# A hybrid decoder block on one core: the instruction order is planned from revised estimates of durations

## The chip, the core and the metric

The kernel runs on one core of a Trainium2 chip. The core's engines work side by side, each taking its own instructions strictly in program order: TensorE (PE) multiplies matrices and transposes, VectorE (DVE), ScalarE (ACT) and GpSimd (POOL) work elementwise, SyncE (SP) issues the DMA transfers. An instruction whose operands are not there yet holds up everything behind it on its engine. The metric is the device time of one execution in microseconds (us), as a median over runs.

## What is computed

One decoder layer, batch 1, 1024 tokens, model width 1024, all float32. Both token mixers read one normed input through one projection:

```python
xn = rms_norm(x, norm1_g)
q, k, v, p_rw = jnp.split(xn @ w_in, [512, 1024, 1536], axis=-1)   # p_rw: 1792 columns
attn = dilated_attention(q, k, v, q_norm_g, k_norm_g)    # 8 heads of 64; windows 128, 512, 2048 at dilation 1, 4, 16
attn = rms_norm(attn, attn_out_g)                        # per head
rwkv = rwkv7_time_mix(p_rw, ...)                         # 8 heads of 64
x = x + jnp.concatenate([attn, rwkv], axis=-1) @ w_out
xn2 = rms_norm(x, norm2_g)
return x + (silu(xn2 @ w_gate) * (xn2 @ w_up)) @ w_down  # 2816 hidden columns
```

The recurrent mixer is, per head and token, `state = state * w + (state·a) b + v k`, `y = state·r`. The dilated attention normalizes q and k (QK-norm), adds a linear bias, and joins three bands by their maxima and sums.

## The kernel before

**Arithmetic.** Matrix products take operands split in a high and a low part (names ending in h and l or hi and lo), so that one float32 product is three passes at the faster rate: `mm<-xn10h,inhi`, `xn10l,inhi`, `xn10h,inlo`.

**Stages.** (1) The start, 0 to 125 us: x is loaded in eight tiles `xt`, squared, normed, transposed (`norms`), and the first blocks of the in-projection (`inproj`, tiles `mm`) are made; `feed` takes each block's sums out: `wa` and `gl` for decays and gates, `stage` for the recurrence's r, k, v, and `sqf` (squares), `qs` (scaled copy), `exf` (the norm's factors, spread) and `vf` for q, k, v. (2) 125 to 567 us: the recurrence goes through the tokens block by block as matrix products; `chain` carries the state `S` from block to block (tiles `Rb`, `VS`, `Ub`; PE results in the `chain` banks), `invert` and `scoring` prepare its matrices, and the rest of the in-projection fills PE between. `post` turns the chain's `Y` into the mixer's output and stores it to DRAM as `mix_d`. (3) 567 to 855 us: attention; q, k, v go through DRAM (`qh_d`, `ql_d`, `kh_d`, `kl_d`, `v_d`) and each head's `qv`, `kk`, `vv` and `bias` are loaded again, seven attend workers make scores (`kk,qv`), softmax (`sb`) and PV products (`pt`), and the out-projection (`outproj`, 16 steps, weights `woraw` split into `woh`, `wol`) uses them: its first round takes the recurrent half, loaded as `mixr` from `mix_d`; the residual `acc` and the second norm (`norms2`, `T1h`, `T1l`) follow. (4) From 855 us the FFN (`gates`, `hidden`, `down`).

**What sets the order.** No order is written by hand. Every operation is handed by a generator (a "stream" with a rank) to a planner, the class `Flow`. It keeps an estimated clock for each engine and an estimated end for each buffer's last write and reads. `scan` gives each operation a cost from its engine and shape; `ready` works out when its operands are there (the end of the writer plus `LAG` of the writer's engine); `run` takes again and again the stream whose next operation is ready first, ties by rank, and `issue` advances the engine's clock and emits it. All instructions are emitted in one line, 229 (`op.fn(*op.a, **op.k)`), so the line tells nothing in the trace and groups are told apart by the names of tiles. The estimates have no effect on the chip but through the order, and through which of a pool's buffers or PSUM banks a tile gets. Banks are handed out by `Get` and given back by `Free` in the planned time. Streams are run in four parts: `flow.run(rwkv)` with the recurrence and the input side, `flow.run(dense)` with the last in-projection, then attention with the out-projection, then the FFN. A stream of a later part can't be emitted before the earlier part is planned to its end; the loads of `woraw`, `mixr` and `acc` come after the last store of `mix_d`. SP has a queue of its own in the plan: 475 ns for an issue, and the bytes at 360 per ns behind each other.

Of the kernel before, what the change touches and what calls it, by code (L numbers as in the profile page):

```python
# [44 lines left out]
NFIX = C_MASK  # L45


LAG = {"PE": 200, "ACT": 145, "DVE": 140, "POOL": 65, "SP": 900}

OWN = {"PE": 0, "ACT": 100, "DVE": 130, "POOL": 95, "SP": 900}  # L50


# [4 lines left out]
class Op:  # L57


    def __init__(self, eng, name, fn, a, k):  # L60
        self.eng, self.name, self.fn, self.a, self.k = eng, name, fn, a, k
# [40 lines left out]
class Flow:  # L102
# [4 lines left out]
    def __init__(self):  # L107
        self.now, self.clk, self.marks, self.streams = 0.0, {}, {}, []
        self.slots, self.keys, self.count, self.shared = {}, {}, {}, set()
        self.free, self.weights = {}, 0.0  # L110

    def tile(self, pool, shape, dtype, name, tag=None, bufs=1):
        tag = tag or name
# [13 lines left out]
    def scan(self, op):  # L127

        def size(ap):
            n = 1  # L130
            for d in ap.shape[1:]:
                n *= d
            return n

        args = [("out" if i == 0 else "in", v) for i, v in enumerate(op.a)] + list(op.k.items())
        aps = [(k, v) for k, v in args if hasattr(v, "tensor")]
        op.wr = [self.keys[v.tensor.name] for k, v in aps if k in ("out", "accum_out") and v.tensor.name in self.keys]
        op.rd = [self.keys[v.tensor.name] for k, v in aps if k not in ("out", "accum_out") and v.tensor.name in self.keys]
        op.wr += [k for k in op.rd if k[0] in self.shared]
        n = max(size(v) for k, v in aps)  # L140
        ptr = sum(hasattr(op.k.get(k), "tensor") for k in ("scale", "bias", "scalar", "scalar1"))
        if op.eng == "PE":
            if op.name == "transpose":
                op.cost, op.m = 110, 128
            else:
                n, m, k = size(op.k["out"]), size(op.k["lhsT"]), op.k["lhsT"].shape[0]
                passes = 1 if op.k["lhsT"].dtype != F32 else PASSES if max(m, k) <= 64 else 4
                op.cost, op.m = 0.4167 * n * passes + 3, m
        elif op.eng == "SP":
            op.cost = 0  # L150
            op.bytes = 4 * max(size(v) * v.shape[0] for k, v in aps)
        elif op.eng == "POOL":
            op.cost = (280 if op.k.get("op") == ALU.pow else 100) + 93 * ptr + n * (168 if op.k.get("op") == ALU.pow else
                                            {"tensor_tensor": 2.15, "tensor_copy": 3.4}.get(op.name, 1.1))
        elif op.eng == "ACT":
            op.cost = 95 + 0.83 * n + 93 * ptr + 91 * ("accum_out" in op.k)
        else:
            op.cost = 65 + 1.04 * n + 64 * ptr

    def advance(self, s):  # L160
        while s.head is None and not s.done:
# [14 lines left out]
    def ready(self, s):  # L176
# [11 lines left out]
        for keys, which in ((op.rd, 0), (op.wr, 0), (op.wr, 1)):  # L188
            for k in keys:
                if k in self.slots:  # L190
                    for e, t in self.slots[k][which].items():
                        if e != op.eng or (e == "SP" and (keys is op.rd or which)):
                            r = max(r, t + LAG[e] + (60 if op.eng == "PE" else 0))
                        elif keys is op.rd and which == 0:
                            r = max(r, t + OWN[e])
        return r

    def issue(self, s, r):
        op = s.head
        s.head = None  # L200
        if isinstance(op, Wait):
            return
        if isinstance(op, Get):
            free = self.free[op.kind]
            s.gift = sorted(free, key=free.get)[:op.n or 1]
            for tag in s.gift:
                del free[tag]
            if op.n is None:
                s.gift = s.gift[0]
            return  # L210
        start = max(r, self.now)
        if op.eng == "SP":
            self.clk["SP"] = start + 475
            end = max(start + 1125, self.clk.get("queues", 0.0)) + op.bytes / 360
            self.clk["queues"] = end
        else:
            if op.eng == "PE":

                start = max(start, self.weights + 0.833 * op.m)
                self.weights = start  # L220
            self.clk[op.eng] = end = start + op.cost
        for keys, which in ((op.rd, 1), (op.wr, 0)):
            for k in keys:
                self.slots.setdefault(k, ({}, {}))[which][op.eng] = end
        s.t = end + (LAG["SP"] if op.eng == "SP" else 0)
        self.emit(op)
# [1611 lines left out]
```

## Time and profile before

| | us |
|---|---|
| runs | 1501.85, 1491.08, 1494.26 (median 1494.26) |
| profiled execution | 1502.63 |
| its span in the trace | 1500.8 |
| its mean granted PE clock | 0.986 of full speed |
| PE busy / weight loads / DVE / ACT / POOL | 1420.0 / 1142.2 / 803.8 / 712.8 / 541.8 |
| 24737 instructions, DMA 173.83 MB | mean 116 GB/s |

The profiled execution lies above the median of the runs and at the upper end of them. A busy time is the sum of an engine's instructions, with overlaps counted once, so span minus busy time is the time in which the engine did nothing, for whatever reason. "Idle before ... <-releaser" names the instruction or transfer whose end came last before an engine went on.

### The profile page before, as it was taken

How to read it: one execution, taken by the hardware profiler on the slowest of the kernel's cores; microseconds unless marked ns; L12 is line 12 of the kernel's file. 1: busy time of each engine (PE TensorE's matmuls, PEld its weight loads, DVE VectorE, ACT ScalarE, POOL GpSimd, SP SyncE). 2: the span in 40 equal slices, each digit the busy share in tenths (PEclk: the TensorE clock that was granted, in tenths of full speed). 3: DMA queues.
4: the chain of work that ended last, by engine and by line, in shares of the span. 5: the costliest groups of instructions: out<-in, count | busy, mean ns of one | idle time of the engine just before them, and what ended most of it. 6: DMA issues, size and time to landing. Idle time of an engine off the chain costs nothing.

```text
span 1500.8 us, 24737 instructions
## 1 busy us (share of the span) xinstructions
PE 1420.0 (95%) x8710; PEld 1142.2 (76%) x8710; DVE 803.8 (54%) x1795; ACT 712.8 (47%) x1764; POOL 541.8 (36%) x564
## 2 busy tenths in 40 slices
PE   8899999999898998899899799999999999999999
PEld 6666766677676776788777688888888888888887
DVE  4456577765655345667687744344443444334334
ACT  6434646556667766557666533333333333333332
POOL 5432344345454455133436734444444440000000
PEclk9899999999999999999999899999999999999999
DMA  6242232331422338996813222222222223445443
GB/s 201 85 128 65 67 82 78 79 96 54 126 82 89 104 116 255 249 243 159 197 37 106 73 90 83 79 78 79 79 82 85 78 85 134 147 146 198 148 147 127
DMA packets 199789, 173.83 MB, mean 116 GB/s; under 512 B 39025, under 2 KB 150897, under 8 KB 199666
## 3 DMA queue, kind: packets, MB, share of 16 engines
q1 hardware_dynamic: 199666, 172.26, 38.7%
q8 instruction: 69, 1.13, 0.3%
q14 instruction: 54, 0.44, 0.1%
HBM read 130.26 MB, written 37.75 MB: 112 GB/s over the span
## 4 chain that ended last, share of the span: by engine, by line
PE 54%; DMA 4%; DVE 3%; SPq 1%; ACT 1%; issue 1%; POOL 0%; ACTq 0%; POOLq 0%; DVEq 0%
PE bank L229 26%; PE mm L229 15%; PE chain L229 13%; DMA kk<-kl_d 2%; SPq L229 1%; DMA bias<-in_tab_dram 1%; DMA qv<-qh_d 1%; DVE acc L229 1%; DMA acc<-in_x_dram 0%; DMA mixr<-mix_d 0%; DVE tt L229 0%; DVE ml L229 0%; DVE T1l L229 0%; DVE nxn L229 0%; POOL ro L229 0%
## 5 line engine op out<-in xcount | busy, mean ns | idle before, releaser
L229 ACT ACTIVATE oph<-fraw 128x512 fp32r<-128x512 f32 x208 | 126.6, 628 | 223.4 <-PE bank L229 117.6
L229 POOL TENSOR_TENSOR opl<-fraw,oph 128x512 fp32r<-128x512 f32 x76 | 101.4, 1336 | 210.6 <-PE bank L229 110.2
L229 DVE TENSOR_TENSOR opl<-fraw,oph 128x512 fp32r<-128x512 f32 x132 | 87.7, 689 | 143.3 <-ACT oph L229 143.3
L229 ACT ACTIVATE oph<-sw 128x512 fp32r<-128x512 f32 x80 | 50.6, 632 | 178.0 <-DVE sw L229 71.9
L229 POOL TENSOR_TENSOR inlo<-inraw,inhi 128x512 fp32r<-128x512 f32 x62 | 82.1, 1325 | 110.6 <-ACT inhi L229 101.0
L229 PE MATMUL bank<-oph 128*128 128x512 f32 x176 | 68.5, 389 | 0.0
L229 PE MATMUL bank<-opl,oph 128*128 128x512 f32 x176 | 68.5, 389 | 0.0
L229 PE MATMUL bank<-oph,opl 128*128 128x512 f32 x176 | 68.5, 389 | 0.0
L229 DVE TENSOR_TENSOR opl<-sw,oph 128x512 fp32r<-128x512 f32 x80 | 56.0, 701 | 18.7 <-ACT oph L229 18.7
L229 DVE SCALAR_TENSOR_TENSOR S<-chain,ec,Sp 64x64 f32<-64x64 f32 x112 | 31.6, 282 | 51.0 <-PE chain L229 40.9
L229 DVE TENSOR_TENSOR uu<-mm,uu 128x512 f32<-128x512 f32 x20 | 13.8, 692 | 81.4 <-PE mm L229 81.4
L229 ACT ACTIVATE Ub<-chain 64x64 f32<-64x64 f32 x128 | 28.2, 220 | 56.7 <-DVE VS L229 54.9
L229 POOL TENSOR_TENSOR sw<-fraw 128x512 f32<-128x512 f32 x40 | 51.9, 1298 | 0.0
L229 ACT ACTIVATE Y<-chain 64x64 f32<-64x64 f32 x128 | 27.2, 214 | 49.2 <-DVE S L229 36.2
L229 ACT ACTIVATE inhi<-inraw 128x512 fp32r<-128x512 f32 x62 | 38.7, 624 | 14.9 <-PE mm L229 7.0
L229 DVE COPY Rb<-chain 64x64 f32<-64x64 f32 x128 | 28.9, 226 | 27.9 <-PE chain L229 25.6
L229 POOL TENSOR_TENSOR up<-up,sg 128x512 f32<-128x512 f32 x20 | 32.5, 1627 | 30.0 <-POOL sw L229 16.0
L229 ACT ACTIVATE sb<-sb,mx 128x256 f32<-128x256 f32 (+3 forms) x64 | 36.3, 569 | 7.9 <-DVE mx L229 7.5
L229 POOL TENSOR_TENSOR rsf<-smf,nhalf 128x8 f32<-128x8 f32 x16 | 27.3, 1708 | 32.3 <-DVE smf L229 26.2
L229 PE MATMUL chain<-Rb,M 128*128 128x128 f32 x128 | 27.8, 299 | 11.7 <-DVE Rb L229 11.5
L229 PE MATMUL bank<-ra,kb 64*64 64x128 f32 x512 | 38.7, 277 | 0.0
L229 PEld LDWEIGHTS chain<-Rb,M 128*128 128x128 f32 x128 | 21.0, 188 | 23.2 <-DVE Rb L229 18.9
(485 smaller groups left out, 4219.4 us busy)
## 6 DMA issues: line engine op xcount, KB each, us to landing
fraw<-in_w_down_dram SPq DMA_DIRECT2D x88, 256.0 KB, 2.8
inraw<-in_w_in_dram SPq DMA_DIRECT2D x62, 256.0 KB, 3.0
fraw<-in_w_gate_dram SPq DMA_DIRECT2D x48, 256.0 KB, 3.7
fraw<-in_w_up_dram SPq DMA_DIRECT2D x48, 256.0 KB, 3.0
fraw<-h_d SPq DMA_DIRECT2D x44, 256.0 KB, 2.9
h_d<-up SPq DMA_DIRECT2D x42, 256.0 KB, 2.1
rkv_d<-stage SPq DMA_DIRECT2D x24, 256.0 KB, 2.3
xt<-in_x_dram SPq DMA_DIRECT2D x8, 512.0 KB, 7.2
```

Source lines behind the costliest of these rows:

```text
L229: op.fn(*op.a, **op.k)
```

## The change

`LAG["SP"]`, the time from a transfer's planned end until a reader may start, goes from 900 to 1500 ns. A new `SWITCH` of 100 ns is charged to PE when a product on the whole array (more than 64 rows and columns, and every transpose) follows one that isn't, or the other way round; it is charged when the operation is issued, and isn't looked at when streams are compared. Products in one pass cost 0.4375 ns for a column of the result instead of 0.4167. An ACT operation whose output has four dimensions (the regrouped copies of q, k, v) costs 1.9 ns for an element instead of 0.83. DVE's fixed part goes from 65 to 80 ns and its rate from 1.04 to 1.08, but 2.2 for scans and 2.0 for four dimensions.

```diff
-LAG = {"PE": 200, "ACT": 145, "DVE": 140, "POOL": 65, "SP": 900}
+LAG = {"PE": 200, "ACT": 145, "DVE": 140, "POOL": 65, "SP": 1500}
+SWITCH = 100
...
-        self.free, self.weights = {}, 0.0
+        self.free, self.weights, self.whole = {}, 0.0, True
...
             if op.name == "transpose":
-                op.cost, op.m = 110, 128
+                op.cost, op.m, op.whole = 110, 128, True
...
-                op.cost, op.m = 0.4167 * n * passes + 3, m
+                op.cost, op.m, op.whole = (0.4375 if passes == 1 else 0.4167) * n * passes + 3, m, min(m, k) > 64
...
-            op.cost = 95 + 0.83 * n + 93 * ptr + 91 * ("accum_out" in op.k)
+            rate = 1.9 if len(op.a[0].shape) == 4 else 0.83
+            op.cost = 95 + rate * n + 93 * ptr + 91 * ("accum_out" in op.k)
         else:
-            op.cost = 65 + 1.04 * n + 64 * ptr
+            rate = {"tensor_tensor_scan": 2.2}.get(op.name, 2.0 if len(aps[0][1].shape) == 4 else 1.08)
+            op.cost = 80 + rate * n + 64 * ptr
...
                 start = max(start, self.weights + 0.833 * op.m)
-                self.weights = start
+                if op.whole != self.whole:
+                    start += SWITCH
+                self.weights, self.whole = start, op.whole
```

Both kernels hold the same instructions: 7336 for PE, 1797 for DVE, 1454 for ACT, 569 for POOL and 898 for SP. Their order differs nearly everywhere up to the FFN, and hardly from there on. Three places follow.

The first is on PE near the end of the in-projection. `mm` is a block of the in-projection, `sqf` its squares made by ACT, `bank<-cs,sqf` their transposes (`cs` holds the identity). Before:

```order
L229 MATMUL mm_6421<-xn11h,inlo 128x512 x4
L229 MATMUL bank_6523<-cs,sqf_6489 128x128 x2
L229 MATMUL bank_6519<-cs,vf_6517 128x128 x4
L229 MATMUL bank_6523<-cs,sqf_6489 128x128 x2
L229 MATMUL mm_6525<-xn10h,inhi 128x512 x4
```

Now, from the end of the same block on:

```order
L235 MATMUL mm_6383<-xn11h,inlo 128x512 x2
L235 MATMUL mm_6481<-xn10h,inhi 128x512 x2
L235 MATMUL chain_6422<-Rb_115,M 128x128
L235 MATMUL mm_6481<-xn10h,inhi 128x512 x2
L235 MATMUL mm_6481<-xn10l,inhi 128x512 x4
L235 MATMUL bank_6499<-cs,sqf_6482 128x128 x4
```

The squares' transposes followed the last product of their own block at once; now eight products of the next block and one of the chain stand between.

The second is on PE from there to the first product on `mixr`, which opens the out-projection. `exf` is the spread norm factor of k, `woh` and `wol` are the out-projection's weights, and the chain's last product stands further ahead. Before:

```order
L229 MATMUL bank_6571<-cs,exf_6551 128x128 x4
L229 MATMUL mm_6525<-xn11l,inhi 128x512 x3
L229 MATMUL mm_6525<-xn11h,inlo 128x512 x4
L229 MATMUL bank_6618<-cs,mixr 128x128 x4
L229 MATMUL chain_6620<-cs,vf_6615 128x128 x4
L229 MATMUL chain_6636<-cs,mixr 128x128 x4
L229 MATMUL bank_6646<-woh_6511,mh 128x512
```

Now, from the chain's last product (`Ub,M`) on; `kk,qv` are scores of attention heads:

```order
L235 MATMUL chain_6422<-Ub_117,M 128x128
L235 MATMUL mm_6481<-xn11l,inhi 128x512 x4
L235 MATMUL mm_6481<-xn11h,inlo 128x512 x3
L235 MATMUL bank_6532<-cs,exf_6517 128x128 x4
L235 MATMUL mm_6481<-xn11h,inlo 128x512
L235 MATMUL bank_6561<-cs,vf_6559 128x128 x4
...
L235 MATMUL chain_6652<-kk,qv 128x256 x2
L235 MATMUL bank_6659<-kk,qv 128x512 x2
L235 MATMUL chain_6640<-kk,qv 128x384
L235 MATMUL mm_6666<-kk,qv 128x256 x2
L235 MATMUL chain_6640<-kk,qv 128x384
L235 MATMUL mm_6688<-cs,mixr 128x128 x4
```

The chain's last product moved into the middle of the last block of the in-projection, and scores of the first two heads (on 4096 columns, with three rows left out here) moved ahead of the first `mixr` product.

The third is on SP at the same place: the stores and loads in the order of issue. Before:

```order
L229 DMA kh_d<-qh_6453 128x512
L229 DMA mix_d<-Y 128x2x128
L229 DMA kl_d<-qs_6359 128x512
L229 DMA kk<-kl_d 64x512 x2
L229 DMA bias<-in_tab_dram 128x512
L229 DMA woraw<-in_w_out_dram 128x512 x5
L229 DMA v_d<-v_6532 128x2x256
L229 DMA v_d<-v_6533 128x2x256
L229 DMA mixr<-mix_d 128x512 x2
L229 DMA woraw<-in_w_out_dram 128x512
L229 DMA kh_d<-qh_6589 128x512
```

Now:

```order
L235 DMA v_d<-v_6472 128x2x256
L235 DMA v_d<-v_6473 128x2x256
L235 DMA kh_d<-qh_6548 128x512
L235 DMA kl_d<-qs_6486 128x512
L235 DMA mix_d<-Y 128x2x128
L235 DMA woraw<-in_w_out_dram 128x512 x5
L235 DMA mixr<-mix_d 128x512 x2
L235 DMA v_d<-v_6593 128x2x256
L235 DMA v_d<-v_6594 128x2x256
L235 DMA vv<-v_d 128x4x128
```

The last stores of k and the last but one of v moved ahead of the store of `mix_d`; between it and the load of `mixr` only the five loads of `woraw` are left. Further on, two loads of `acc` moved behind one head's loads, and the next five of `woraw` behind those of two more heads.

## Rows read from the trace of the kernel before

**Rows 1.** Page, part 1: busy us, share, instructions of each engine.

```profile
PE 1420.0 (95%) x8710; PEld 1142.2 (76%) x8710; DVE 803.8 (54%) x1795; ACT 712.8 (47%) x1764; POOL 541.8 (36%) x564
```

**Rows 2.** Stages: us, busy PE PEld DVE ACT POOL (instructions), PE clock, DMA share, GB/s.

```profile
0.00:125.00 125.00, 113.00 (x765) 82.02 (x766) 63.07 (x117) 57.37 (x101) 51.94 (x75) 0.93 0.43 131
125.00:567.00 442.00, 412.22 (x3639) 318.06 (x3638) 272.14 (x707) 274.65 (x849) 197.43 (x204) 1.00 0.30 87
...
584.00:815.00 231.00, 204.92 (x1283) 176.06 (x1284) 165.01 (x526) 144.26 (x421) 85.59 (x131) 0.97 0.68 180
815.00:855.00 40.00, 32.42 (x138) 25.43 (x137) 35.41 (x38) 24.83 (x44) 33.25 (x26) 0.87 0.22 66
855.00:1500.00 645.00, 642.10 (x2817) 528.58 (x2816) 259.68 (x395) 204.38 (x337) 164.11 (x123) 1.00 0.34 109
```

**Rows 3.** Waits of PE, 100 to 570: us in total, times, longest us.

```profile
PE chain L229 <- DVE Rb L229: 11.5, 15, 1.6
PE chain L229 <- ACT Ub L229: 4.0, 9, 0.8
PE bank L229 <- ACT sqf L229: 2.6, 5, 1.0
...
PE bank L229 <- ACT vf L229: 2.0, 4, 0.8
```

**Rows 4.** Waits of PE, 570 to 860.

```profile
PE bank L229 <- DMA mixr<-mix_d: 5.5, 1, 5.5
PE bank L229 <- DVE T1l L229: 3.3, 1, 3.3
PE mm L229 <- ACT first L229: 3.0, 1, 3.0
```

**Rows 5.** Timeline at 211: start us, us, instruction [idle before <-releaser].

```profile
211.36 0.30 PEld L229 LDWEIGHTS chain<-S,ra 128*128 128x128 f32 x2 [0.17 <-issue]
```

**Rows 6.** Timeline of PE in the start.

```profile
42.25 0.67 PE L229 MATMUL bank<-cs,xt 128*128 128x128 f32 x4 [2.07 <-DVE xt L229]
42.85 2.07 PE L229 MATMUL bank<-wa,w2a2s 64*128 64x512 f32 x2
```

**Rows 7.** Groups of ACT: count | busy us, mean ns | idle before.

```profile
L229 ACT ACTIVATE sqf<-mm 128x512 f32<-128x512 f32 x16 | 17.2, 1078 | 5.0 <-PE mm L229 4.5 <-issue 0.3
```

**Rows 8.** Timeline of PE at the handover to attention.

```profile
576.28 0.44 PE L229 MATMUL bank<-cs,sqf 128*128 128x128 f32 x2 [1.15 <-ACT sqf L229]
...
589.44 1.09 PE L229 MATMUL bank<-cs,mixr 128*128 128x128 f32 x4 [5.46 <-DMA mixr<-mix_d]
```

**Rows 9.** Chain that ended last, 560 to 590: start us, us, what.

```profile
563.72 0.44 PE bank L229 x4
...
566.45 0.24 PE chain L229 x2
566.69 4.33 PE mm L229 x19
...
582.96 6.35 DMA mixr<-mix_d
```

**Rows 10.** Timeline of SP's issues there.

```profile
576.58 0.38 SPq L229 DMA_DIRECT2D mix_d<-Y  x1
...
579.35 2.33 SPq L229 DMA_DIRECT2D woraw<-in_w_out_dram  x5
...
582.96 1.33 SPq L229 DMA_DIRECT2D mixr<-mix_d  x2
```

**Rows 11.** Windows in attention, columns as in rows 2.

```profile
580.00:590.00 10.00, 4.54 (x23) 3.56 (x22) 3.58 (x5) 5.49 (x9) 4.98 (x4) 0.94 1.01 314
590.00:600.00 10.00, 10.00 (x56) 8.98 (x55) 6.34 (x27) 7.37 (x21) 3.06 (x3) 0.88 0.85 276
680.00:760.00 80.00, 72.33 (x487) 63.41 (x486) 57.19 (x199) 54.29 (x167) 33.92 (x64) 0.96 0.69 166
720.00:730.00 10.00, 8.16 (x39) 7.59 (x39) 3.94 (x15) 3.99 (x12) 3.75 (x10) 0.66 0.97 229
```

## The prediction, made before the changed kernel ran

> **What bounds the kernel now.** I read the busy times first, then the stages, then the waits of TensorE (PE) stage by stage, then the chain that ended last around the places where the order changes. PE is busy for 1420.0 of the profiled execution's 1500.8 us, the next engine for 803.8 [rows 1]. So the kernel is bound by PE's work plus PE's holes, and a reordering that leaves the work as it is can move only the holes: 1500.8 − 1420.0 = 81 us at most, 5.4% of the time. The stages show where they lie [rows 2]: 12.0 us in the start (0 to 125 us), 29.8 in the recurrence (125 to 567), 26.1 in attention (584 to 815), 7.6 in the tail before the FFN (815 to 855), and only 2.9 in the FFN's 645 us. In the recurrence the holes belong to the chain of state products: PE waits 11.5 us in 15 places for Rb and 4.0 in 9 for Ub, and besides it 2.6 for sqf and 2.0 for vf [rows 3]. One wait of 5.5 us, for mixr, stands at the handover to attention, and in the tail there are 3.3 us for T1l and 3.0 for first [rows 4].
>
> **The change, part by part.** Nothing is added or removed: the same products, vector operations and transfers run, in another order. The new estimates have no cost on the chip. What is priced is where the order puts a wait.
>
> *FFN, from 855 us: 0.* Its order is practically the old one, and with 642.1 of 645.0 us busy [rows 2] no hole is left to shift.
>
> *Switches between 64-row and whole-array products: 0.* There are 162 on PE in the old order, 164 in the new. The row bounds one: the weights of a whole product after four small ones waited 0.17 us [rows 5], so two more cost less than 0.4 us. Below nothing isn't possible, as there are more of them.
>
> *Start: 0.* Here PE waits 2.07 us for xt at 42.25, and runs wa,w2a2s right after [rows 6]. The new order has the norms ahead of wa's Tanh on ScalarE (ACT), so the wait for xt goes and one for wa of about the same length comes in its place. Bounds: −2 (the old wait goes and none comes) to +4 (the new one is twice as long and in front of all that follows).
>
> *Feeds of q, k and v: −5.* An operation that squares or copies 512 columns in the regrouped 4-D form takes 1078 ns [rows 7]; the old table gives 95 + 0.83 × 512 = 520, the new one 95 + 1.9 × 512 = 1068. So the old order put the transposes of sqf and vf on PE too early: 9 of 16 times less than 1.4 us of other PE work stands between the product and the transposes of its squares, once nothing (the first order piece); in the new order it is 2 of 16, and for vf 1 of 8 instead of 7. The waits are 2.6 + 2.0 [rows 3] and the one of 1.15 at 576.28 [rows 8], 5.8 in all; one short place is left for vf and two for sqf, which I put at 0.8. Bounds −5.8 to 0.
>
> *The chain, 125 to 567: +4.* The longer estimates of the vector engines pull chain products apart in some places and crowd them in others. Adding up the PE work that covers each of the chain's steps, the mean rises (1.06 to 1.12 us ahead of the Rb product, 1.52 to 1.65 ahead of VS), but the thin places too: below 0.7 us 9 → 13 of 64 for Rb, below 0.9 us 7 → 12 of 64 for Ub, below 1.4 us 11 → 15 of 60 for S. At the mean wait of Rb and Ub in the rows (11.5 / 15 = 0.77 and 4.0 / 9 = 0.44 us [rows 3]), and S taken as Ub, that is 4 × 0.77 + 5 × 0.44 + 4 × 0.44 = 7.0; the thicker mean takes part of it back, and I keep about half. Bounds: +8, and −8 if the thicker mean halves the 15.5 us of these waits.
>
> *Handover to attention: +9.* This is the clearest change in the order. The chain's last product starts at 566.45 and the mixr product at 589.44 [rows 8, 9]; between them the old order has nearly the whole last in-projection (4.33 us for 19 products, 0.228 each [rows 9]), so PE is covered until 5.46 us before mixr lands. In the new order the chain's last product stands in the middle of the last mm block: behind it come 8 mm products (1.8 us), two groups of transposes (0.44 each [rows 9]), and then score products on 4096 columns (8 × 0.228 = 1.8), that is 4.5 us. The path to mixr itself: from the last chain product to the store of mix_d is 576.58 − 566.69 = 9.9 us; the store's own issue takes 0.38, the 5 issues of woraw that now follow it 2.33 [rows 10], and mixr lands 6.35 us after its issue [rows 9], 19.0 in all. 19.0 − 4.5 = 14.5 us of hole, against 5.5 before: +9. Bounds: 0, if the vector work behind the chain's end is shorter because fewer feeds stand in it; and +14, if mixr waits for mix_d's landing rather than for the queue: from 576.58 to 582.96 [rows 10] were 6.4 us, 3.7 more than my 2.7; and 1.8 for the scores, if their operands, which come through the same full queues (share 1.01, [rows 11]), are late and they cover nothing. What waits behind mixr on PE is the rest of the scores and the out-projection; nothing else can run, since the engine takes its instructions in order.
> The Trainium skill (DMA: Bandwidth & Descriptors, Anatomy of one DMA — SWDGE path) gives a transfer a fixed 2.0 us and 436 GB/s, an estimate of 2.6 us for mixr's 256 KB. The trace disagrees, with 6.35 us here [rows 9], so its term of about +5 in place of +9, and a sum of 1486, is not taken.
>
> *Attention and out-projection, 584 to 815: −8.* Scores start earlier: 59 us of PE work stand behind the last score product up to the norms instead of 44.5, so the heads' loads are spread over more time. Between 680 and 760 the 16 queues are idle for 31% of 80 us = 25 us [rows 11], while at 710 to 730 PE stands for the loads of the next head. The acc loads and the second five of woraw are behind two heads' loads in the new order. I take a third of the 25 us. Bounds: −25, and +10, when thinner covers count (median PE work ahead of the PV transposes 2.40 → 2.09 us, ahead of the sb ones 4.84 → 4.27: a tenth to an eighth less cover for 26 us of holes is +3, and I allow three times that).
>
> *Tail, 815 to 855: −4.* The first norm transposes stand 10 us of PE work earlier than in the old order, which is cover for the 7.6 us of holes there [rows 2], 6.3 of which are the two waits [rows 4]; half. Bounds −7.6 to 0.
>
> Sum: 0 + 0 + 0 − 5 + 4 + 9 − 8 − 4 = **−4 us**. The profiled execution took 1502.6 us, above the runs' median of 1494.26 (1491.08 to 1501.85); the difference carries over to the median: **1490 us**.
>
> **The rivals.**
> *Attention was paced by its loads, and is released (faster).* Speaks for it: the queues' 25 idle us between full stretches [rows 11], PE at 8.16 of 10 us in 720 to 730 with DMA at 0.97. Against: 205 of 231 us are PE work already [rows 2], so all 25 would have to come from the loads. Then −5 + 4 + 9 − 25 − 4 = −21, **1473 us**.
> *The long hole at the handover and thin covers (slower).* The mechanism is one: score and chain work that covered the handover now stands ahead of it. Where PE stood, the granted clock fell: 0.94 and 0.88 in the two stretches around the 5.5 us wait, 0.66 in 720 to 730 [rows 11], which is time at 1.2 instead of 2.4 GHz. In 590 to 600 a mean of 0.88 means 2.4 us at the lower level, some 1.2 us lost. The price: feeds −5, chain +4, handover +14, attention's covers +5, and 2 for the clock of a longer hole, with nothing from the tail: +20, **1514 us**. It decides if the hole at the handover is 15 us or more and attention gives nothing back.
> The Trainium skill (TensorE: Matmul & The Clock Gate, HAM oscillation) names the same: an idle PE drops to half clock and the next products start slow; the rows quoted show it.
> *The change doesn't do what it says.* The order is set by estimates, and PE waits by real latencies. If the new places of the feeds only turn waits for sqf into waits for chain products, −5 and +5 cancel, the handover's +9 stands against −8 of attention, and if the tail gives nothing either it is +1, **1495 us**. It lies within the forecast's case.
>
> **How the numbers follow.** Forecast and "no net change": 0.55 (0.05 of it the third rival). Faster rival 0.25, slower rival 0.20. A measurement of this kernel tells about 1% (15 us) from no change, so these are also the chances of faster, same and slower. The likeliest case's own range is 1480 to 1508. The range to be given reaches into the cases at both ends: 1473 is the released attention, 1512 just short of the slower one's whole price, which leaves out about 2 in 10.
>
> **What would show it.** Right: waits of PE for sqf and vf down from 5.8 to about 1; waits for Rb and Ub together at about 19 instead of 15.5; a hole of 12 to 16 us before the mixr product, with a granted clock under 0.9 behind it; FFN of 645 us as before; attention a little shorter, its last score product earlier. Wrong: if the hole at the handover stays near 5 us the term was too big and the time falls to some 1481; if these two fall below 11 us the covers were judged badly; if the FFN's length moves, nothing in this account explains it.

## The result

The changed kernel takes 1504.49 us as a median of 20 runs (1495.98 to 1509.59), the kernel before 1495.36 (1486.80 to 1506.00, 20 runs): a ratio of 1.0051 with a 95% interval of 1.003 to 1.0071. A second set of runs gave 1505.59 and 1496.04, 1.0076 (1.005 to 1.0102). So by its ratios it is some 8 to 11 us slower, clear of zero and inside what I had called "no change". The range held it; the sign was wrong, since 4 us of gain were forecast. Of the 89 runs of the kernel before that were made beside the experiments, one took 2297.60 us at a granted clock of 0.554 and is left out below.

The profiled execution of the changed kernel took 1504.73 us (span 1502.7). Its busy times answer to [rows 1], its stages to [rows 2]; columns are the same.

```profile
PE 1425.6 (95%) x8710; PEld 1147.0 (76%) x8710; DVE 805.3 (54%) x1795; ACT 710.4 (47%) x1764; POOL 537.3 (36%) x564
```

```profile
0.00:125.00 125.00, 112.78 (x707) 81.38 (x708) 60.74 (x115) 55.44 (x97) 52.65 (x75) 0.93 0.43 131
...
567.00:584.00 17.00, 11.84 (x61) 9.52 (x59) 8.01 (x19) 6.73 (x15) 3.89 (x3) 0.88 0.59 179
584.00:815.00 231.00, 208.33 (x1262) 174.49 (x1263) 162.76 (x523) 141.77 (x417) 81.62 (x131) 0.94 0.65 176
815.00:855.00 40.00, 32.67 (x140) 25.76 (x139) 35.12 (x37) 24.22 (x43) 30.66 (x24) 0.89 0.22 66
855.00:1500.00 645.00, 643.64 (x2819) 529.07 (x2817) 259.06 (x396) 204.89 (x338) 164.40 (x123) 1.00 0.34 108
```

The last row's window is a little later in the program than before, so it isn't the same work word for word, but two things stand out. PE is busy 5.6 us longer for the same products, with 3.7 us less of holes in the span; and the granted clock of attention is 0.94 instead of 0.97.

Waits of PE, as in [rows 3] (100 to 575 us), then as in [rows 4] (570 to 870), and last the waits for sb of the kernel before in 570 to 870:

```profile
PE chain L235 <- DVE Rb L235: 9.0, 13, 1.8
PE chain L235 <- ACT Ub L235: 8.0, 10, 1.8
```

```profile
PE mm L235 <- ACT sb L235: 5.7, 4, 3.4
PE mm L235 <- DMA mixr<-mix_d: 5.0, 1, 5.0
PE bank L235 <- DVE T1l L235: 3.4, 1, 3.4
PE bank L235 <- ACT first L235: 3.0, 1, 3.0
PE bank L235 <- ACT vf L235: 2.3, 1, 2.3
PE bank L235 <- DVE v L235: 2.0, 1, 2.0
...
PE bank L235 <- ACT sb L235: 1.8, 6, 0.5
PE chain L235 <- ACT sb L235: 1.8, 4, 0.7
```

```profile
PE mm L229 <- ACT sb L229: 0.9, 1, 0.9
...
PE bank L229 <- ACT sb L229: 0.6, 1, 0.6
```

The waits for sqf are gone and those for vf are one; the waits in the tail haven't moved. Waits for sb, attention's softmax, have grown from 1.5 to 9.3 us. The handover on PE, as in [rows 8], and on SP, as in [rows 10]:

```profile
577.15 0.66 PE L235 MATMUL bank<-cs,vf 128*128 128x128 f32 x4 [2.27 <-ACT vf L235]
...
580.86 1.19 PE L235 MATMUL bank<-kk,qv 128*128 128x512 f32 x2 [2.02 <-DVE v L235]
...
588.08 1.11 PE L235 MATMUL mm<-cs,mixr 128*128 128x128 f32 x4 [4.95 <-DMA mixr<-mix_d]
```

```profile
579.53 0.37 SPq L235 DMA_DIRECT2D mix_d<-Y  x1
580.00 2.33 SPq L235 DMA_DIRECT2D woraw<-in_w_out_dram  x5
582.37 1.21 SPq L235 DMA_DIRECT2D mixr<-mix_d  x2
```

Behind the chain's last product stood holes of 1.2, 0.4 and 5.5 us; now there are three of 9.2 us together, with 4.0 us of PE work between the first and the `mixr` product.

**Where the 9 us come from.** Windows cut at the same work, not at the same time, answer that: from the start of the first `mixr` product to the end of the last product of the second norm (`nxn`), which takes in all of attention and the out-projection. First the two profiles of the kernel before: that of [rows 1], and a second one (below), of a run 3 us above its median; then the changed kernel's. Columns as in [rows 2].

```profile
589.40:841.10 251.70, 228.00 (x1392) 194.61 (x1393) 183.54 (x543) 157.85 (x445) 104.22 (x147) 0.97 0.63 165
590.10:836.70 246.60, 229.39 (x1392) 195.86 (x1393) 182.47 (x543) 157.84 (x445) 104.16 (x147) 0.96 0.63 169
```

```profile
588.10:841.70 253.60, 232.04 (x1373) 193.73 (x1374) 181.61 (x531) 156.07 (x441) 100.07 (x147) 0.95 0.60 162
```

Against the second profile the changed kernel is ahead by 2.0 us up to this window (588.1 against 590.1), though the in-projection ends 9 to 10 us earlier (574.9 against 584.0 and 584.7 in the two profiles). In the window it takes 7.0 us more, and 19 products fewer stand in it. The rest, behind it, is 1.3 us longer. The first profile of before has 1.9 us less than the changed kernel in this window, so single profiles bound the loss there only loosely; the experiments below settle it.

### The profile page after: what moved, and what is told of

It is laid out like the page before. It is cut to its first block, busy times and chain, and to the rows that moved or that the text cites. A ratio compares the mean times of both kernels' runs of the same rounds, so it can differ in the third digit from the quotient of the medians.

```text
span 1502.7 us, 24763 instructions
## 1 busy us (share of the span) xinstructions
PE 1425.6 (95%) x8710; PEld 1147.0 (76%) x8710; DVE 805.3 (54%) x1795; ACT 710.4 (47%) x1764; POOL 537.3 (36%) x564
## 5 line engine op out<-in xcount | busy, mean ns | idle before, releaser
L235 DVE TENSOR_TENSOR up<-chain,uu 128x512 f32<-128x512 f32 x40 | 27.7, 692 | 29.7 <-PE chain L235 29.7
L235 PEld LDWEIGHTS bank<-oph 128*128 128x128 f32 x176 | 33.0, 188 | 6.9
L235 PEld LDWEIGHTS bank<-opl,oph 128*128 128x128 f32 x176 | 33.0, 188 | 6.8
L235 PEld LDWEIGHTS bank<-oph,opl 128*128 128x128 f32 x176 | 33.0, 188 | 6.8
```

## Experiments

All ratios are to the kernel before on the same chip. "Attention window" is the window just described; "first round" is the out-projection's first round, which uses the recurrent half. Positions "in us of PE work" come from adding up the products of the planned order, as in the prediction.

**A second look at both kernels.** The kernels as they are.

> The changed kernel as it is, beside the others on the same chip. Both theories expect what was measured: 1.005 of the kernel before (1.003 to 1.007), a mean granted clock about 0.98 against 0.986 in the profile of before. Theory C (clock): in its profile PE's busy time is about 5 us above that of before, with fewer holes. Theory H (holes): holes make up the difference.

> The kernel before, once more, for a second profile of it: the first was of an execution 7 us above the median of its runs. 1.000. If the in-projection again ends near 584 us, the changed kernel's end of it at 575 is a gain of 9 us that is lost later; if it ends near 578, the gain is some 3 us and so is what is lost later.

Measured: 1.0076 (1.005 to 1.0102) for the changed kernel; 0.9981 (0.9954 to 1.0008) for before against itself. In-projection's end 575.5 and 584.7, so its earlier end is not luck of one profile. Attention windows 253.1 against 246.6; in the first profile of before it was 251.7, 5.1 us more, about the 4.4 us by which that execution was longer than the second. In these profiles holes are equal (74.8 and 75.0 us over the span); what grew is PE's busy time, 1428.1 against 1421.4 us, which is nearer to theory C than to H. Half of that is the clock: PE was busy for 49.3 us at the lower level, 1.2 GHz, against 42.7, and half of such time is lost, 3.3 us of the 6.7.

**Idle products at the handover.** The order is that of the change; dummies are put in when an instruction is emitted.

```diff
     def emit(self, op):
+        if op.eng == "PE":
+            self.n = getattr(self, "n", -1) + 1
+            for _ in range(FILL.get(self.n, 0)):      # {3088: 18, 3098: 16, 3106: 40}
+                self.pe.transpose(out=op.k["out"][:, 0:128], in_=self.ident, identity=self.ident)
         op.fn(*op.a, **op.k)
```

> The changed kernel with 74 idle transposes of the identity put in front of three products at the handover, where PE waits for vf (18), for a bank (16) and for mixr (40); the planned order of all else is the same. The dummies' results are overwritten. Theory C (PE's clock falls to 1.2 GHz where it stands at the handover, and the products behind it run slow): the half-clock stretch of 580.0 to 593.7 us with 7.9 us of busy PE goes, the granted clock of 580 to 595 is near 1, and the time falls by 3 to 5 us against the changed kernel (1.002 of before). Theory H (only the waits count): clock may rise, the time stays within 1 us of the changed kernel (1.005), since the scores and mixr arrive when they did.

Measured: 1504.07 us, 1.0062 (1.0035 to 1.009). Windows from the in-projection's end to `mixr` and the 6 us behind it, first of the changed kernel (second profile), then with the dummies:

```profile
575.50:588.90 13.40, 3.98 (x19) 3.22 (x19) 7.68 (x25) 6.33 (x15) 3.92 (x4) 0.67 0.63 207
588.90:594.90 6.00, 6.00 (x26) 5.24 (x27) 3.98 (x12) 4.95 (x13) 2.16 (x2) 0.59 1.10 380
```

```profile
576.50:589.90 13.40, 11.03 (x93) 10.27 (x91) 7.42 (x22) 6.08 (x14) 3.66 (x4) 1.00 0.66 202
589.90:595.90 6.00, 5.66 (x36) 4.27 (x37) 4.76 (x16) 5.99 (x17) 2.45 (x2) 1.00 1.11 381
```

The clock did what was meant, 1.00 in place of 0.67 and 0.59. The handover kept its 13.4 us, since the path to `mixr` sets it, and the attention window went from 253.1 to 251.9, without and with dummies:

```profile
588.90:842.00 253.10, 233.44 (x1373) 194.22 (x1374) 180.95 (x528) 155.61 (x438) 99.80 (x147) 0.95 0.61 162
```

```profile
589.90:841.80 251.90, 229.19 (x1373) 190.78 (x1374) 181.34 (x531) 155.89 (x440) 100.19 (x147) 0.97 0.61 163
```

PE was busy 4.3 us less for the same products, but stood 3.0 us longer: what the clock gave back went mostly into waits. The time fell by 1.5 us in the medians, which these intervals can't tell from nothing; theory C expected 3 to 5, theory H at most 1. PE's clock at the handover is a minor part.

**Parts of the change alone, or left out.** Kernel before with one part, or the changed kernel without one.

```diff
# e1_rates_only = before +                       # e1_lag_only = before +
+ rate = 1.9 if ... 4-D (ACT)                    + LAG["SP"] 1500
+ DVE 80 + 1.08 n, scans 2.2, 4-D 2.0
# e2_pe_only = before + 0.4375, SWITCH = 100
# e2_no_act  = changed, ACT 0.83 throughout      # e2_no_dve = changed, DVE 65 + 1.04 n
```

> The kernel before with the new ACT and DVE durations alone (4-D ACT 1.9 ns, DVE 80 + 1.08 n, scans 2.2, 4-D 2.0). Theory A (the durations gave the earlier end of the in-projection, 584.0 to 574.9 us, and LAG the loss in attention): in-projection ends 5 to 9 us earlier than before, attention as before, time 0.995 to 0.998 of before. Theory B (the loss comes with the durations, since the chain's last product moves into the last block of the in-projection): PE's hole at the handover 9 us or more, time 1.003 to 1.006.

> The kernel before with LAG of SP at 1500 instead of 900 and nothing else. Theory A: loads and their readers move apart in attention, out-projection weights behind heads' loads; its first round ends late (about 745 instead of 704 us) and PE stands longer at the handover, time 1.004 to 1.008 of before, sqf and vf waits as before. Theory B: no difference beyond 0.2%.

> Only the PE part of the change: 0.4375 ns for a column and SWITCH. In its order the chain's last product has 41 us of in-projection behind it (15 before, 2 in the changed kernel), and, as in the changed kernel, the last PV product stands ahead of the out-projection's second round (558 against 560 us of PE work; before 581 against 532). Theory D (the handover's hole is the loss): no wait for mixr, time 0.994 to 0.998 of before. Theory O (out-projection left for the end, so that attention's products stand alone and thin): from the first score to the last norm product 4 to 8 us longer than before, time 1.000 to 1.005.

> The changed kernel without the ACT rate of 1.9. Chain's cover at the handover as before (15 us of PE work), sqf and vf transposes early again (waits 4 to 6 us), out-projection's second round late as in the changed kernel (559 against a last PV at 560). Theory D: 0.998 to 1.001 of before. Theory O: 1.003 to 1.006, as the changed kernel.

> The changed kernel without the new DVE durations. 25 us of cover at the handover, sqf and vf transposes late, out-projection and attention mixed nearly as before (second round from 544, last PV at 575). Theory D and theory O: both 0.993 to 0.998 of before. If it is 1.003 or more, both fall, and the cause is in the recurrence.

| kernel | ratio (95%) | mean clock of its runs | in-projection's end | first mixr | attention window |
|---|---|---|---|---|---|
| before (second profile) | 1 | 0.987 | 584.7 | 590.1 | 246.6 |
| changed | 1.0076 (1.0050 to 1.0102) | 0.979 | 575.5 | 588.9 | 253.1 |
| LAG only | 0.9995 (0.9976 to 1.0015) | 0.984 | 575.8 | 588.1 | 247.3 |
| ACT and DVE only | 1.0115 (1.009 to 1.014) | 0.968 | 536.1 | 606.3 | 247.9 |
| PE part only | 1.0133 (1.0091 to 1.0175) | 0.988 | 594.9 | 565.5 | (291.7) |
| changed without ACT | 1.0108 (1.0068 to 1.0148) | 0.982 | 586.4 | 596.3 | 256.6 |
| changed without DVE | 1.0092 (1.0059 to 1.0125) | 0.982 | 597.8 | 600.2 | 258.4 |

Of the expectations little was left. LAG alone does nothing, and the ACT and DVE durations alone lose 1.2% in the recurrence: the in-projection is used up 56 us ahead of the chain's end (536.1 against 591.9; 48 us earlier than in the kernel before), and the chain then runs nearly alone, with a granted clock of 0.56 from 536 to 606 and a wait of 9.8 us for `mixr`; attention is as before. The PE part alone loses 1.3% with the best clock of this table and only 1.9 us of wait for `mixr` (its window holds work of the in-projection too, so it isn't comparable). That speaks against theory D, the handover as the loss. Theory O, attention's order as the loss, was to cost up to 0.5%; the kernel came out at 1.3, but the in-projection ends 10 us later in it, so not all of that is attention's. Both kernels with a part left out are slower than the whole change and lie above what either theory gave; the parts don't add up, because each moves the order everywhere. By the sign set down for the kernel without DVE, both theories should fall: the second round starts 44 us ahead of the last PV product there, where the changed kernel has 17, and yet its window is 258.4 us. So how late the out-projection comes isn't enough to tell the time of an order.

**One half of the program at a time.** All new estimates up to `flow.run(dense)` and the old ones behind it, and the reverse. The order up to the handover is then that of the changed kernel, or of before, word for word.

```diff
     flow.run(dense)
+    flow.table(False)    # old estimates from here on; e3_old_then_new: the reverse
```

> The new estimates up to the end of the in-projection, the old ones from there on (attention, out-projection, FFN); the order up to the handover is that of the changed kernel word for word. In its order the out-projection's second round starts at 540 us of PE work, 37 ahead of the last PV product (before 532 and 49, changed 555 and 10). Theory O (the loss is in attention's order, where the out-projection comes late and attention's products stand alone): mixr near 588.5 as in the changed kernel, from there to the last product of the norms 247 to 250 us instead of 253, time 0.998 to 1.001 of before. Rival R (the loss is the recurrence and the handover): 1.004 to 1.008 as the changed kernel.

> The other half: the old estimates up to the end of the in-projection, the new ones from there on. The order up to the handover is that of before word for word; in its order the second round starts at 552, 10 ahead of the last PV product. Theory O: mixr near 590 as before, from there to the last product of the norms 252 to 257 us against 247 to 252, time 1.003 to 1.007 of before. Rival R: 0.999 to 1.001.

Measured: new, then old 1488.8 us, **0.9959** (0.9939 to 0.9979), faster than both kernels and better than either theory had it; old, then new 1.0055 (1.0035 to 1.0076), as theory O had it. Attention windows 238.0 and 248.8, of 247 to 250 and 252 to 257 expected. The two, to be held against the changed kernel's row above:

```profile
588.60:826.60 238.00, 223.49 (x1372) 190.23 (x1373) 180.64 (x531) 156.34 (x440) 100.86 (x147) 0.97 0.63 172
```

```profile
590.50:839.30 248.80, 233.60 (x1391) 197.73 (x1392) 184.93 (x544) 157.38 (x445) 100.51 (x147) 0.95 0.62 167
```

In the first the same order leads up to the window and one product fewer is in it, but it is 15.6 us shorter than in the changed kernel: 8.6 less of busy PE, 7.0 less of holes. So the new estimates do harm in attention, and up to the handover they are worth something, though most of that gain shows behind it: the first `mixr` product comes 1.5 us earlier than in the second profile of before, the window is 8.6 us shorter and has 20 products fewer, most of them scores that went ahead of `mixr`. Rival R is rejected by the times from both sides; the second kernel's window alone, 2.2 us above that of before in one profile, wouldn't show it.

The mean clock of the first kernel's runs, 0.980, is as low as the changed kernel's 0.979, but over the whole program much of the low clock falls on holes and on the recurrence. In the window the granted clock is 0.97 against 0.95: PE is busy at the lower level for 12.4 us against 22.0, and half of the difference, 4.8 us, is the clock's part of the 8.6. No run tells whether the order would cost as much at an equal clock.

**More of the out-projection early.** `flow.add(9.5, outproj())` at 8.1.

> The changed kernel with the rank of the out-projection's stream at 8.1 instead of 9.5, so that at equal times its products go ahead of attention's; estimates as in the change. First round ends at 490 us of PE work instead of 553. Theory O: with out-projection products spread through attention there is more cover, from mixr to the last product of the norms 246 to 251 us, time 0.998 to 1.002 of before. Rival R: as the changed kernel, 1.004 to 1.008. If attention gets longer, out-projection products in its way cost more than they cover.

Measured: 1542.96 us, 1.0326 (1.0304 to 1.0347). The first round ends at 650 us of the trace instead of 746, and attention is much longer: from `mixr` to the last norm product 287.1 us, with waits for sb and pt of 7.8 and 5.1 us. Every theory had it at 1.008 or less. "Out-projection late" is therefore too simple as a cause: hurried, its products cost more than they cover.

**Which estimate in attention.** From `flow.run(dense)` on the old estimates and SWITCH; or all the new ones without SWITCH; or SWITCH at 0 throughout.

```diff
     flow.run(dense)
+    flow.table('switch')                        # e4_att_switch
+    flow.table('col', 'act', 'dve', 'lag')      # e4_att_noswitch
-SWITCH = 100
+SWITCH = 0                                      # e4_switch0
```

> All new estimates up to the end of the in-projection; from there on the old ones, but with SWITCH of 100 ns. Theory S (SWITCH alone makes attention's order slow: it is charged to PE's planned clock for each change between PV products on 64 columns and the rest, and the out-projection is left for last; first round ends at 559 us of PE work, the last PV product stands at 557): 8 to 15 us above the same kernel without SWITCH there (0.9959 of before), so 1.001 to 1.006 of before; from mixr to the last product of the norms 250 us or more against 238. Theory W (the whole set together does it, no part alone): within 3 us of the kernel without, 0.995 to 0.998.

> The changed kernel with SWITCH left out from the end of the in-projection on, all else new throughout. In its order the first round ends at 529, the last PV product at 582. Theory S: 0.993 to 0.999 of before, 238 to 246 us from mixr to the last product of the norms. Theory W: 1.003 to 1.007, as the changed kernel.

> The changed kernel with SWITCH at 0 throughout. First round ends at 538, last PV product at 578; but in the recurrence the order changes too, with the chain ending at 436 us of PE work, 3 behind the end of the in-projection. Theory S: attention 238 to 246 us; the recurrence's end and the handover lose 3 to 8 us; 0.995 to 1.002 of before. Theory W: 1.003 or more.

Measured: with SWITCH alone in attention 1.0164 (1.0143 to 1.0185), 2% above the same kernel without it (0.9959); all but SWITCH 1.0028 (1.0012 to 1.0044); SWITCH at 0 throughout **0.9965** (0.995 to 0.998), faster than before. The attention windows are 263.4, 249.4 and 244.4 us. With SWITCH alone, the same window and the first of PE's waits:

```profile
589.40:852.80 263.40, 235.27 (x1372) 195.33 (x1373) 184.87 (x529) 155.89 (x439) 100.28 (x147) 0.93 0.58 156
```

```profile
PE chain L240 <- POOL wol L240: 8.1, 4, 3.8
```

Against 238.0 us it has 11.8 us more of busy PE and 13.6 more of holes, and the out-projection waits for its own second weights (`wol`) between 757 and 770 us, behind the last PV product at 752.6. (8.7 of the 11.8 us are the clock, 0.93 against 0.97.) Theory S holds here, and twice as large as I had put it. In the changed kernel it holds for less than half: without SWITCH in attention it takes 1.0028 instead of 1.0051 and 1.0076, which is 0.2 to 0.5% better, but short of the 0.993 to 0.999 that theory S gave and just outside theory W's 1.003 to 1.007. The other new estimates cost about 0.7% in attention too (1.0028 against 0.9959); which of them was not tried.

**SWITCH and the price of a column alone, in the kernel before.**

> The kernel before with SWITCH of 100 ns and nothing else. Its order ends the first round of the out-projection at 559 us of PE work (before 528), with the last PV product at 558 (before 581). Theory S: 1.008 to 1.018 of before, most of it behind the handover (over 255 us from the end of the in-projection to the last product of the norms, with PE idle over 30), although the chain now ends 36 us of PE work ahead of the in-projection's end. If it is within 0.3% of before, SWITCH hurts only together with the other estimates.

> The kernel before with 0.4375 ns for a column in place of 0.4167 and nothing else. First round ends at 548, last PV product at 569: between before and SWITCH alone. Theory S (the price of a change of array use, not that of a column, is what moves attention the wrong way): 0.998 to 1.005 of before, below half of what SWITCH alone costs.

Measured: SWITCH alone 1533.23 us, 1.0219 (1.0171 to 1.0267); the column's price alone 1496.56, 0.9992 (0.9962 to 1.0022). The PE part's loss is SWITCH. It is more than the 1.008 to 1.018 expected, and a good part of it lies ahead of attention: in the profile the in-projection ends at 596.6 us, 12 later than before, and 272.1 us follow up to the last norm product instead of 257.1 and 252.0.

That any new order could be faster or slower by chance is a rival that one pair can't answer. Five pairs here differ in SWITCH alone, and in all five the kernel with it is slower: by 2.2% in the kernel before, 1.4% beside the column's price (1.0133 against 0.9992), 2.0% in attention on the old estimates, 0.2 to 0.5% in attention on the new ones, and 0.9 to 1.1% in the changed kernel throughout (1.0051 and 1.0076 against 0.9965). Only the 0.2 of these is within the noise.

**Idle products in the tail.** The fastest kernel (new, then old), with 28 dummies ahead of a block behind which PE waits for `first`, and 36 ahead of T1h; the same lines as above with `FILL = {4432: 28, 4484: 36}`.

> The kernel with new estimates up to the handover and old ones behind it (0.9959 of before), with 28 idle transposes ahead of the last chain block of the first gate columns and 36 ahead of the T1h products, where PE then waits 3.1 us for first, and 1.2 and 3.3 for T1h and T1l. The dummies do no work that is needed and end before what PE waits for. Theory C (half clock behind a hole costs half of the busy time in it, where PE is the bound): the half-clock stretches of 820.7 to 824.2 and 834.4 to 841.2 with 9.3 us of busy PE go, and the time falls by 4 to 4.7 us, to 0.992 to 0.994 of before. If the clock costs nothing there: 0.996.

Measured: 1488.57 us, 0.9958 (0.994 to 0.9977), no different from 0.9959. In the profile the place itself gains. From the end of the last norm product on, 20 us and then all up to PE's last product, without and with dummies:

```profile
826.60:846.60 20.00, 15.44 (x55) 11.83 (x54) 14.64 (x17) 8.99 (x16) 14.16 (x11) 0.83 0.22 65
826.60:1482.80 656.20, 651.64 (x2845) 535.72 (x2843) 271.50 (x409) 211.51 (x349) 175.03 (x131) 0.99 0.33 107
```

```profile
832.20:852.20 20.00, 19.05 (x102) 16.00 (x102) 15.49 (x19) 9.42 (x17) 15.41 (x12) 1.00 0.26 77
832.20:1485.80 653.60, 652.64 (x2881) 537.41 (x2880) 271.47 (x409) 211.32 (x349) 175.18 (x131) 1.00 0.33 108
```

The clock went from 0.83 to 1.00 and the rest of the program from 656.2 to 653.6 us, of 4 to 4.7 expected. The medians don't show these 2.6 us: they are inside the interval of 3, and 0.9958 is where the clock was to cost nothing. So the clock's price is seen in one profile and not settled by the runs.

## What SWITCH charges, and what the chip charges

The planner calls a product whole if rows and columns of its weights are both over 64, so it charges 100 ns where 128 rows by 64 columns follow 128 by 128. PV products come in such pairs: 136 with weights of 128 columns and 136 with 64, in turn. By that rule there are 456 changes on PE in the order of before and 454 in the changed one, counted over all that the planner issues, and some 270 of them are PV's, 27 us of planned PE time in attention. On the chip, PV products of both forms in turn (the row names the first form), on 256 columns:

```profile
615.01 0.63 PE L235 MATMUL chain<-pt,vv 128*128 128x256 f32 x4
615.47 0.88 PE L235 MATMUL bank<-kk,qv 128*128 128x256 f32 x4
```

Four start and the next thing follows 0.46 us later: 0.115 each, and 0.227 for 512 columns of an unswitched product is 0.114 for 256. There is no price. Over all pairs of the trace of before, where the clock was full, the median from a 128*128 start to its 128*64 partner's is 62 ns for 128 columns and 118 ns for 256, and back from 128*64 to 128*128 60 and 119; between products of 256 columns that are all 128*128 it is 120. A change to weights of 64 rows and 64 columns does cost:

```profile
212.04 0.62 PE L235 MATMUL mm<-xn0h,inhi 128*128 128x512 f32 x2
212.59 1.09 PE L235 MATMUL bank<-ra,kb 64*64 64x128 f32 x16
```

Two products of 512 columns take 0.55 us up to the small ones instead of 0.455; the median of 15 such places in the trace of before is 327 ns for the last one instead of 227, and it is 327 too ahead of weights of 64 rows and 128 columns (9 places). So 100 ns is right for the change to 64 rows, and PV's charges, more than half of all, are for nothing.

The Trainium skill (TensorEngine Tiling (Array Packing), Key Properties) says that changing the tiling mode, not just the tile, drains TensorE. The rows agree for 64*64, with 0.1 us; for 128*64 behind 128*128 they show no such cost.

Why a charge for nothing moves attention is read in `ready` and `run`: an operation's time is the later of its operands and its engine's planned clock. Where PE's clock runs ahead of all operands, all of PE's streams are ready at the same time, and the rank decides, attend's 8.2 before the out-projection's 9.5. The orders show it: with SWITCH alone from the handover on the first round ends at 559 us of PE work, without at 537, in the changed kernel at 553, in before at 528. That the planned clock does this is argued from the code and these positions; no run took the ranks away. A rule that charges for rows alone (`k > 64`) was not run under that name: the order it gives is, word for word on every engine, that of the kernel without SWITCH in attention, measured at 1.0028. The mended charge by itself thus still doesn't beat the kernel before.

## Why the prediction was wrong, point by point

- **FFN 0.** Right within 1.3 us (656.0 and 657.3 us from the last norm product to PE's last one).
- **Switches 0.** Right as a cost on the chip, since the number of changes hardly moves: 456 and 454 by the change's own rule. I had counted 162 and 164, and so missed PV's. What I didn't look at is what the charge does to the plan: 27 us of PE time in attention that the chip doesn't take. Its effect belongs in the terms of attention and the tail below.
- **Start 0.** Right: 12.2 us of holes against 12.0, clock 0.93 in both.
- **Feeds −5.** Mechanism right: 5.8 us of waits for sqf and vf have become 2.3, one wait at the handover. −3.5.
- **The chain +4.** Rb and Ub together are 17.0 and 16.0 us in the two profiles of the changed kernel, 15.5 and 16.9 in those of before; I said 19. No change is shown.
- **Handover +9.** Too large, and its mechanism only in part right. From the chain's end to the first `mixr` product PE stands 9.2 us, against 7.0; without the waits for sqf and vf, which the feeds hold already, that is 7.0 against 5.5: +1.5, and about 1 for the clock (PE is busy 2.3 us at the lower level there, and not at all before). The cover was larger than forecast (6.2 us, part of it at half clock, against 4.5) and the path shorter: from the last chain product to `mixr` 572.6 to 588.1, 15.5 us instead of 19.0, because the store of `mix_d` came after 7 us rather than 9.9 and `mixr` was there 5.7 us after its issue. The figure that I set beside it from the Trainium skill (DMA: Bandwidth & Descriptors, Anatomy of one DMA — SWDGE path) stands there for transfers issued by GpSimd. `mixr` is issued by SP, so its 5.7 us speak against my use of the figure and not against the page. By my own sign a hole that stays near 5 us meant a time of some 1481. The wait for `mixr` is 5.0 us and the time rose, so the error that decides lies behind it.
- **Attention −8 and tail −4.** The step that failed, and it sets the sign. From the first `mixr` product to the last norm product the changed kernel needs 253.6 and 253.1 us in two profiles, before 251.7 and 246.6: +1 to +7 instead of −12. I had taken the −8 from the heads' loads, and no release of them is shown: PE's waits for `kk` are 9.6 and 3.6 us in the two profiles of before, 4.6 and 5.2 in those of the changed kernel. What grew in its place is the wait for softmax, 1.5 and 0.8 us for sb before, 9.3 and 5.9 now. The last PV product does end 4 to 10 us earlier (768.6, against 773.0 and 779.0), as I read from the order. But what is left then is more: the second round starts at 751.5, 17 us ahead of that, where it had 62 to 66, and 73 us follow the last PV product instead of 62 to 64. I had called that cover for the tail. The tail's waits need work between their producer and their consumer, and they stayed at 3.4 and 3.0 us. My reading is that the out-projection's products had been the cover of attention's, and that without them attention's own stand more alone: between the first profiles, 2.7 us more in PV products and 2.8 in sb's transposes, each taken up to the next product's start, at the same count and the clock taken out. That this is waiting that the trace counts as busy is argued; what the halves and the pairs above show is that the new estimates behind the handover cost it, SWITCH the most of the parts tried. I had bounded thin covers at +10 by 26 us of holes and left the middle at −8.
- **Luck.** The terms up to `mixr` added up to +8 and came to −1.3 and −2.0 us (588.1 against 589.4 and 590.1). So two errors of opposite sign partly cancel, and that the range held is partly luck: 10 us more up to `mixr`, with the same attention, would have been some 1514, just beyond it.
- The rival of a released attention is out: the heads' loads were not what paced it. The slower rival named a long hole, thin covers and the clock, at 1514; the hole isn't longer (5.0 us of its deciding 15), thin covers and a lower clock are there, and its price was twice too high. The third rival, 1495, had the feeds' gain cancelled by the chain; the feeds did gain, and attention gave nothing.
- The clock, which I had in the slower rival alone: over 88 runs of the kernel before, time and mean granted clock go together (correlation −0.85, 11 us for 0.01). Which drives which isn't shown. It isn't what parts the two profiles of before: the longer one has the higher clock (0.986 and 0.984), and 6.0 us more of waits for `kk`. Between kernels it explains less still: PE's part alone has 0.988 and is 19 us slower than before, the fastest kernel has 0.980.

What stays open: which of LAG, column price, ACT and DVE costs the 0.7% in attention when SWITCH is gone, how much of an order's price is the clock, and what fills attention best.

## To carry to other kernels

A planner's estimates act through order alone: price an added charge by where and how often the plan applies it, not only by what the chip takes for it, and look at what each low-priority stream was covering before you count its later place as cover. Test a change of estimates by halves of the program; here the new estimates in the first half alone were worth −0.4%, in the second alone +0.6%, and the whole showed neither. A rule copied to all engines' operations should be measured at the most frequent form it meets.

## What the runs showed of the hardware

Changing from 128 by 128 weights to 128 by 64 and back costs nothing that can be read (62 and 118 ns for 128 and 256 columns either way), while 64 by 64 behind 128 by 128 costs 0.1 us. It goes by the rows of the weights: 64 by 128 costs the same 0.1 us. And one and the same kernel's runs spread over 1.3% (1486.7 to 1505.9 us in 88 runs), going together with their granted clock. Idle products in a hole lift the clock behind it (0.67 to 1.00 and 0.83 to 1.00), but the program gained no more than 1.5 us by it in the medians.
